# An attention and Fourier block: the Fourier stage's sums taken once for both halves of the frequencies, and one set of weight sums handed from VectorE to accumulating transfers

## The chip, the cores and the metric

The kernel runs on one core of a Trainium2 chip. A core has engines that run side by side, each with its own queue of instructions: TensorE (PE in the profile) multiplies matrices and writes to PSUM, which has eight banks of 128 partitions by 512 words; VectorE (DVE) and ScalarE (ACT) work element by element; GpSimd (POOL) and SyncE (SP) here mostly issue transfers (DMAs) between the chip's memory and the core's SBUF. The metric is the time of one execution on the device in microseconds (us): the median of several runs.

## The reference

One layer over 512 latent tokens of width 2048, with 256 context tokens:

```python
h = modulate(rmsnorm(x), shift, scale)          # shift, scale, gate from c @ w_ada
p = h @ w_in                                    # 2048 -> 9216
attn = attention(rope(q), [rope(k), kc], [v, vc])
u = u_b.reshape(b, n, 4, 128)                   # 4 groups of 128 channels
y = jnp.fft.fftn(u, axes=(1, 3), norm="ortho").real
y_a = (attn * silu(z_a)) @ w_pa
y_b = (y * silu(z_b)) @ w_pb
out = rmsnorm(x + gate * ((sigmoid(g_a) * y_a + sigmoid(g_b) * y_b) @ w_out)) * final_g
```

The edit is in the Fourier part (`u_b`, `z_b`) and at the start of the large product `h @ w_in`. Of the transform over 512 tokens and 128 channels only the real part is wanted. For a real input, the transforms at frequency f and at 512 − f of the tokens share their sums: with C the sum with cosines and S the sum with sines over the channels, one is C − S and the other C + S.

## The kernel before, in words

**Products in three.** All matmuls are done in single precision as three products of rounded parts. A weight tile of 128x1024 words is split by `split_from` (L181, L182): ScalarE copies it, rounded, into the high half (`hi`), and VectorE subtracts that from it for the low half (`lo`). `mm3` (L339 to L341) then issues high by high, high by low and low by high. The split of a tile must be done before its matmuls start; TensorE's order is fixed by the code in the stages spoken of here, and the order on the other engines is set by the scheduler of the framework, except where `issue_after` or `behind` names an instruction that must stand ahead. `look` says how many tiles are split ahead of their use.

**The stages.** A start stage, to about 144.5 us, makes the modulated rows of `h` and the columns of `u_b` and `z_b`. Then comes the channel stage (the Fourier part). Then the rest of `w_in` goes in eight groups, 0 to 7, each as seven products in the manner of Strassen, in the order P1, Q5, P2, Q6, P7, Q3, Q4. Each product has four pieces of 12 matmuls, 128x512 each: 48 in all.

**Sums of weights.** P1 needs the block A11 of the weights, Q5 the sum Z5, Q6 the sum S2: each one more addend on the one before. They are kept in four tiles, R0 to R3 (`chain`), one for each piece. A load on SP's queue fills R (L220) for P1. In `split_piece` (L263 and on) the next addend is put in one of two ways. Either the raw addend has been loaded into a buffer `wr`, and VectorE adds it (L269), when the piece is split; or a transfer on POOL's queue adds the addend from memory into R (L292, `accum_op=ALU.add`), as soon as the split before has read R. `BY_DVE_GATES = (1,)` says that step 1, Q5's sums, goes by VectorE; step 2, Q6's, by transfers. The loop over groups that fills the list of pieces hands it on at L429.

**The channel stage.** For each channel group g of four, `tokens(g)` multiplies the half-sums of `u` (`uh`, `ul`) with tables of cosines and sines over the tokens (`fsq`), once for even and once for odd frequencies, and splits the result into `ah`, `al`. `positions(g)` multiplies these with the channels' table `fch` (cos, −sin, sin): one PSUM bank gets 256 columns for the frequencies upward and 256, read backwards, for those downward, by 8 matmuls with `ah` (L940) and 4 with `al` (L943). VectorE multiplies the bank with the gate (L945). `gate_b(g)` makes the gate: ScalarE's Sigmoid of `z` (L950), and VectorE's product of the two (L951). While this goes on, pieces of P1 are split, held by `behind` after `low[g]`, the split of a channel group. The four results go to memory (`b_d`, L967) on POOL's queue. Behind these there, `turning <- rot_d` (L1394) loads the tables of rotations that the first group's queries need.

Of the kernel before, what the change touches and what calls it, by code (L numbers as in the profile page):

```python
# [18 lines left out]
P = 128  # L19
D = 2048  # L20
T = 512
# [25 lines left out]
HL, MORE_HL = 3, 2  # L47
EVEN = 258

# [74 lines left out]
def block_kernel(ctx, tc, xT, ctx_rows, ctx_toks, x, c_row, w_ss, w_gate, vecs, qkg, rope, dft_c, dft_s,  # L124
# [74 lines left out]
    def stream(key, src, *a, **k):  # L199
        todo.append(Piece(key, src if isinstance(src, list) else [src], *a, **k))  # L200
# [57 lines left out]

    last_split, split_of, in_line, context_sub = [], [], [], []

    look = [1]

    def split_piece(e):  # L263
# [27 lines left out]
        if e.nxt is not None:  # L291
            nc.gpsimd.dma_start(chain[e.pc], e.nxt, accum_op=ALU.add)  # L292
        if e.stage == 3:
# [74 lines left out]
    for p in start_pieces():  # L368
        if p[2:5:2] == (KK - 4, 0):
            stream(("dfts", 0), dft_s[:, : 2 * EVEN], 2 * EVEN, 2, "raw")  # L370
            stream(("dftc", 0), dft_c, 3 * P, 1, "raw")
        elif p[2:5:2] == (KK - 4, 4):
            stream(("dfts", 1), dft_s[:, 2 * EVEN :], T, 2, "raw")
        stream(("start", p), w_start[p[0] : p[0] + P * p[1]].rearrange("(p c) -> p c", p=P), p[1], p[2 + 1])
# [139 lines left out]
    with tc.issue_after(nc.scalar.activation(ce, cvt, ACT.Exp, scale=-1.0).ins):  # L514
# [381 lines left out]
    ul = fnp.tile([P, 2, 2, T], F32R, name="ul")  # L896
    fsq.append(fnp.tile([P, 2, 2, 256], F32R, name="fsq1"))
    split_table(1)
# [17 lines left out]

    AH, low = {}, {}

    def tokens(g):

        ah, al = (fnp.tile([P, 2, 257], F32R, tag=n, bufs=2, name=uid(n)) for n in ("ah", "al"))
        c = slice(P * g, P * g + P)
        for e in range(2):
            n = fsq[e].shape[-1]
            acc = bank()
            for a in range(2):
                mm3(acc[:, :n], uh[:, a, e, c], ul[:, a, e, c], fsq[e][:, 0, a, :], fsq[e][:, 1, a, :], a == 0, a == 1)
            k = slice(e, 257 - e, 2)
            low[g] = split_from(acc[:, :n].rearrange("p (r f) -> p r f", r=2), ah[:, :, k], al[:, :, k])[1]
        AH[g] = ah, al  # L930

    def positions(g):

        ah, al = AH.pop(g)
        acc = bank2()
        steps = [(256 * q, P * (r and 1 + q), (slice(0, 256) if q == 0 else slice(256, 0, -1)), r)
                 for q in range(2) for r in range(2)]
        for n, (o, t, k, r) in enumerate(steps):
            for m, i in enumerate((0, 1)):
                nc.tensor.matmul(acc[:, o : o + 256], fch[:, i, t : t + P], ah[:, r, k], start=n == m == 0, stop=False,  # L940
                                 skip_group_check=True)
        for n, (o, t, k, r) in enumerate(steps):
            nc.tensor.matmul(acc[:, o : o + 256], fch[:, 0, t : t + P], al[:, r, k], start=False, stop=n == 3,  # L943
                             skip_group_check=True)
        nc.vector.scalar_tensor_tensor(part[:, 4 + g, :], acc, 1.0 / 256.0, part[:, 4 + g, :], op0=ALU.mult, op1=ALU.mult)  # L945

    def gate_b(g):
        z = part[:, 4 + g, :]
        e = fnp.tile([P, T], F32, tag="sil", bufs=1, name=uid("e"))
        nc.scalar.activation(e, z, ACT.Sigmoid)  # L950
# [12 lines left out]
    ordered.close()  # L963
    look[0] = 2
# [428 lines left out]

    nc.gpsimd.dma_start(turning, rot_d)  # L1394
    for g, kind in enumerate(KINDS):
# [586 lines left out]
def _constants():  # L1982
# [9 lines left out]
    a = 2 * np.pi * (np.outer(np.arange(P), np.arange(P)) % P) / P  # L1992
    dft_c = np.concatenate([np.cos(a), -np.sin(a), np.sin(a)], axis=1).astype(np.float32)

# [4 lines left out]

    dft_s = np.concatenate([table(np.arange(0, T // 2 + 1, 2)), table(np.arange(1, T // 2, 2))], axis=1)  # L2000
    return np.ascontiguousarray(rope), np.ascontiguousarray(dft_c), np.ascontiguousarray(dft_s)
# [60 lines left out]
```

## Time and profile before

| | |
|---|---|
| median of 3 runs | 1290.95 us (1290.47 to 1291.25) |
| profiled execution | 1290.1 us, span 1288.3 us |
| granted TensorE clock, mean | 0.997 |
| TensorE busy | 1271.5 us (99%), 6586 matmuls |
| VectorE busy | 994.8 us (77%) |
| ScalarE busy | 681.1 us (53%) |
| POOL busy | 168.8 us (13%) |
| memory traffic | mean 248 GB/s |
| channel stage | 144.55 to 156.08 us |
| group 0 up to its last product | 156.08 to 223.31 us |

The span is the time from the first to the last record of the profiled execution; its own time includes what lies around that. A busy share of 99% means that nearly every microsecond has a matmul in flight; matmuls overlap, so the pace is read from the distance between starts. The rows give start, busy time, engine, line, operation and the tiles; in brackets stands the time that the engine idled before, and what ended the wait. Tile numbers are left out in the profile.

### The profile page before, as it was taken

The page shows a single profiled execution, that of the slowest core. Times are in us where ns is not written, and L with a number is a line of the kernel's source. Part 1 is how long each engine was busy: PE and PEld are TensorE (multiplying, and loading weights), DVE is VectorE, ACT ScalarE, POOL GpSimd, SP SyncE. Part 2 cuts the span into 40 slices and gives each one's busy share as a digit, 9 for nine tenths or more (in the row PEclk, how much of TensorE's full clock was granted, in tenths as well). Part 3 has the DMA queues.
Part 4 walks back from the last instruction along what each step waited for, and adds up shares of the span by engine and source line. Part 5 has one row for each costly group of instructions (what it writes and reads, how often), then busy time and mean ns, then how long its engine had stood idle before and what let it go on. Part 6 is the DMA issues. An engine that isn't in the chain of part 4 may idle for free.

```text
span 1288.3 us, 17679 instructions
## 1 busy us (share of the span) xinstructions
PE 1271.5 (99%) x6586; PEld 1047.1 (81%) x6586; DVE 994.8 (77%) x1305; ACT 681.1 (53%) x1072; POOL 168.8 (13%) x222
## 2 busy tenths in 40 slices
PE   8999999999999999999999999999999999999997
PEld 5677887888888888888888888888888888888886
DVE  5767899889779787758587666788898767887677
ACT  5322655645456455444354544666667646465544
POOL 0000011111102011012021010012100212211210
PEclk9999999999999999999999999999999999999999
DMA  9999588888899998977879897578852989898986
GB/s 377 411 367 345 207 216 251 246 212 250 210 310 253 297 269 262 294 191 189 271 212 265 284 229 258 182 245 241 267 179 77 248 244 259 243 213 229 225 201 180
DMA packets 104342, 319.14 MB, mean 248 GB/s; under 512 B 9888, under 2 KB 32800, under 8 KB 100288
## 3 DMA queue, kind: packets, MB, share of 16 engines
q1 hardware_dynamic: 54912, 197.40, 42.1%
q0 software_dynamic: 27024, 98.19, 35.6%
q10 hardware_dynamic: 22320, 22.42, 5.1%
q8 instruction: 51, 0.84, 0.2%
q14 instruction: 35, 0.29, 0.1%
HBM read 283.36 MB, written 34.61 MB: 247 GB/s over the span
## 4 chain that ended last, share of the span: by engine, by line
PE 90%; DVE 4%; DMA 3%; ACT 2%; issue 1%; SPq 0%; ACTq 0%; DVEq 0%
PE banks L339 10%; PE banks L340 10%; PE banks L341 10%; PE x L341 8%; PE x L339 8%; PE x L340 8%; PE y L341 7%; PE y L340 7%; PE y L339 7%; PE banks L1543 2%; PE pd L567 2%; PE pb L339 1%; PE pb L341 1%; PE pb L340 1%; PE pc L339 1%; DMA wa<-in_w_ss 1%
## 5 line engine op out<-in xcount | busy, mean ns | idle before, releaser
L181 ACT ACTIVATE whi<-R 128x1024 fp32r<-128x1024 f32 x138 | 145.1, 1058 | 138.7 <-PE banks L341 55.5
L182 DVE TENSOR_TENSOR wlo<-R,whi 128x1024 fp32r<-128x1024 f32 x138 | 167.2, 1220 | 54.4 <-ACT whi L181 54.0
L182 DVE TENSOR_TENSOR wlo<-wr,whi 128x1024 fp32r<-128x1024 f32 (+1 forms) x122 | 147.0, 1211 | 62.3 <-ACT whi L181 62.3
L181 ACT ACTIVATE whi<-wr 128x1024 fp32r<-128x1024 f32 (+1 forms) x122 | 127.4, 1051 | 127.8 <-PE y L341 39.2
L339 PE MATMUL banks<-whi,s 128*128 128x512 f32 (+1 forms) x400 | 157.8, 395 | 0.8 <-ACT ev L1154 0.7
L341 PE MATMUL banks<-whi,s 128*128 128x512 f32 (+1 forms) x400 | 155.9, 390 | 0.0
L340 PE MATMUL banks<-wlo,s 128*128 128x512 f32 (+1 forms) x400 | 155.8, 389 | 0.0
L339 PE MATMUL x<-whi,s 128*128 128x512 f32 x352 | 137.1, 390 | 0.0
L341 PE MATMUL x<-whi,s 128*128 128x512 f32 x352 | 137.0, 389 | 0.0
L340 PE MATMUL x<-wlo,s 128*128 128x512 f32 x352 | 136.9, 389 | 0.0
L339 PE MATMUL y<-whi,s 128*128 128x512 f32 x316 | 123.1, 389 | 0.2 <-DVE cxe L1266 0.2
L340 PE MATMUL y<-wlo,s 128*128 128x512 f32 x316 | 123.1, 389 | 0.1
L341 PE MATMUL y<-whi,s 128*128 128x512 f32 x316 | 122.8, 389 | 0.0
L292 POOL DMA_DIRECT2D R<-in_w_g x64 | 55.9, 873 | 418.8 <-DVE wlo L182 212.8
L181 ACT ACTIVATE s<-wr 128x512 fp32r<-128x512 f32 (+2 forms) x93 | 60.4, 676 | 74.1 <-DMA wr<-cf_d 24.9
L182 DVE TENSOR_TENSOR s<-wr,s 128x512 fp32r<-128x512 f32 (+2 forms) x93 | 66.8, 748 | 35.6 <-ACT s L181 34.7
L339 PEld LDWEIGHTS banks<-whi,s 128*128 128x128 f32 x400 | 75.2, 188 | 16.5 <-ACT ev L1154 1.1
L341 PEld LDWEIGHTS banks<-whi,s 128*128 128x128 f32 x400 | 75.1, 188 | 15.3
L340 PEld LDWEIGHTS banks<-wlo,s 128*128 128x128 f32 x400 | 75.2, 188 | 13.8 <-DVE wlo L182 0.2
L340 PEld LDWEIGHTS x<-wlo,s 128*128 128x128 f32 x352 | 66.1, 188 | 13.7
L341 PEld LDWEIGHTS x<-whi,s 128*128 128x128 f32 x352 | 66.1, 188 | 13.7
L339 PEld LDWEIGHTS x<-whi,s 128*128 128x128 f32 x352 | 66.1, 188 | 13.5
(322 smaller groups left out, 2796.6 us busy)
## 6 DMA issues: line engine op xcount, KB each, us to landing
wr<-in_w_g SPq DMA_DIRECT2D x128, 512.0 KB, 6.0
R<-in_w_g POOLq DMA_DIRECT2D x64, 512.0 KB, 7.7
wa<-in_w_ss SPq DMA_DIRECT2D x31, 1024.0 KB, 9.7
R<-in_w_g SPq DMA_DIRECT2D x32, 512.0 KB, 5.4
wr<-in_w_gate SPq DMA_DIRECT2D x32, 512.0 KB, 5.0
wr<-in_w_o SPq DMA_DIRECT2D x24, 512.0 KB, 7.2
R<-in_w_o POOLq DMA_DIRECT2D x24, 512.0 KB, 9.0
wr<-in_w_pab SPq DMA_DIRECT2D x20, 512.0 KB, 5.8
```

Source lines behind the costliest of these rows:

```text
L181: first = nc.scalar.activation(hi, src, ACT.Copy)
L182: return first, nc.vector.tensor_tensor(lo, src, hi.bitcast(F32), op=ALU.subtract)
L292: nc.gpsimd.dma_start(chain[e.pc], e.nxt, accum_op=ALU.add)
L339: nc.tensor.matmul(o, ah, bh, start=start, stop=False, skip_group_check=cont)
L340: nc.tensor.matmul(o, ah, bl, start=False, stop=False, skip_group_check=cont)
L341: nc.tensor.matmul(o, al, bh, start=False, stop=stop, skip_group_check=cont)
L567: nc.tensor.matmul(acc[32 * j : 32 * j + 32], c2[:, n, :], w[:, k, :], start=n < 4, stop=n >= KK - 4)
L1543: nc.tensor.transpose(tp[:, k * P : (k + 1) * P], p[:, k * P : (k + 1) * P], ident)
```

## The change

- Both token tables have 258 columns (`FREQ`); the odd one had 256.
- `positions` reads all 258 columns once: 3 matmuls into a bank for the sum with cosines, 3 into a second one for the sum with sines (6 in place of 12, each of 258 columns). ScalarE copies the second bank to `odd` (L941). VectorE forms the upward half as a difference (L942, 257 words), and the downward half as a sum of both read backwards (L943, 255 words, written from word 257 on) into `y`. The product with the gate follows later (L961), for two channel groups at a time. The factor 1/256 is in `fch`, which now holds cos and sin.
- The banks are exchanged: `tokens` writes to the tags `b2` and `b3` (two banks each, named `pd` and `pc`), `positions` to `b1` (four banks, `pb`).
- `gate_b` is one Silu on ScalarE (L948); the product of VectorE is gone.
- In group 0, Q5's sums go by accumulating transfers on POOL's queue (L292); their raw loads and VectorE's sums (L269) go there.
- The rotations' load (L1415) is issued in group 0's P2, after the last accumulating transfer issued until then (`chained`).
- For the last two channel groups, pieces are held behind `low[3]`.

```diff
-EVEN = 258
+FREQ = 258
...
         if e.nxt is not None:
-            nc.gpsimd.dma_start(chain[e.pc], e.nxt, accum_op=ALU.add)
+            chained[:] = [nc.gpsimd.dma_start(chain[e.pc], e.nxt, accum_op=ALU.add)]
...
-            stream_product(name, g, w_g[g], BY_DVE_GATES)
+            stream_product(name, g, w_g[g], BY_DVE_GATES if g else ())
...
-    fch = ppool.tile([P, 2, 3 * P], F32R, name="fch")
-    fsq = [ppool.tile([P, 2, 2, EVEN], F32R, name="fsq0")]
+    fch = ppool.tile([P, 2, 2 * P], F32R, name="fch")
+    fsq = [ppool.tile([P, 2, 2, FREQ], F32R, name="fsq0")]
...
-        ah, al = (fnp.tile([P, 2, 257], F32R, tag=n, bufs=2, name=uid(n)) for n in ("ah", "al"))
+        ah, al = (fnp.tile([P, 2, FREQ], F32R, tag=n, bufs=2, name=uid(n)) for n in ("ah", "al"))
...
-            acc = bank()
+            acc = (bank3 if e else bank2)()[:, :FREQ]
...
-        acc = bank2()
-        steps = [(256 * q, P * (r and 1 + q), (slice(0, 256) if q == 0 else slice(256, 0, -1)), r)
-                 for q in range(2) for r in range(2)]
-        for n, (o, t, k, r) in enumerate(steps):
-            for m, i in enumerate((0, 1)):
-                nc.tensor.matmul(acc[:, o : o + 256], fch[:, i, t : t + P], ah[:, r, k], start=n == m == 0, stop=False,
+        acc = [bank()[:, :FREQ] for _ in range(2)]
+        for i, v in ((0, ah), (1, ah), (0, al)):
+            for r, o in enumerate(acc):
+                nc.tensor.matmul(o, fch[:, i, P * r : P * r + P], v[:, r, :], start=i == 0 and v is ah, stop=v is al,
                                  skip_group_check=True)
-        for n, (o, t, k, r) in enumerate(steps):
-            nc.tensor.matmul(acc[:, o : o + 256], fch[:, 0, t : t + P], al[:, r, k], start=False, stop=n == 3,
-                             skip_group_check=True)
-        nc.vector.scalar_tensor_tensor(part[:, 4 + g, :], acc, 1.0 / 256.0, part[:, 4 + g, :], op0=ALU.mult, op1=ALU.mult)
+        z = part[:, 4 + g, :]
+        y, odd = (fnp.tile([P, n], F32, tag=t, bufs=4, name=uid(t)) for t, n in (("y", T), ("odd", FREQ)))
+        nc.scalar.copy(odd, acc[1])
+        nc.vector.tensor_tensor(y[:, :257], acc[0][:, :257], odd[:, :257], op=ALU.subtract)
+        nc.vector.tensor_tensor(y[:, 257:], acc[0][:, 255:0:-1], odd[:, 255:0:-1], op=ALU.add)
+        products.append((z, y))
 
     def gate_b(g):
         z = part[:, 4 + g, :]
-        e = fnp.tile([P, T], F32, tag="sil", bufs=1, name=uid("e"))
-        nc.scalar.activation(e, z, ACT.Sigmoid)
-        nc.vector.tensor_tensor(z, z, e, op=ALU.mult)
+        nc.scalar.activation(z, z, ACT.Silu)
...
-        with behind((finals[-1], low[g])):
+        with behind((finals[-1], low[g if g < 2 else 3])):
             for e in ahead[:g]:
                 split_piece(e)
+            for z, y in products[2 * g - 4 : 2 * g - 2] if g > 1 else ():
+                nc.vector.tensor_tensor(z, y, z, op=ALU.mult)
...
-    nc.gpsimd.dma_start(turning, rot_d)
...
+            if (g, name) == (0, "P2"):
+                with behind(chained):
+                    nc.gpsimd.dma_start(turning, rot_d)
```

Three places in the order of the instructions, of the kernel before and of the changed one. The first is VectorE's, at the end of the channel stage, up to the low half of R3 (`wlo` from R3, P1's fourth piece). `wlo` and `s` are low halves, `Z50`, `Z51` and `S30` are forms of the tokens' rows, `pd` and `pb` PSUM banks. Before:

```order
L182 TENSOR_TENSOR wlo272_1596<-R2_1341,whi271_1595 128x1024
L945 SCALAR_TENSOR_TENSOR part_108<-pd266_1560,part_108 128x512
L269 TENSOR_TENSOR R0_1339<-R0_1339,wr230_1353 128x1024
L945 SCALAR_TENSOR_TENSOR part_108<-pd270_1581,part_108 128x512
L182 TENSOR_TENSOR s280_1667<-Z50_69,s279_1666 128x1024
L182 TENSOR_TENSOR s284_1689<-Z51_70,s283_1688 128x1024
L269 TENSOR_TENSOR R1_1340<-R1_1340,wr231_1359 128x1024
L269 TENSOR_TENSOR R2_1341<-R2_1341,wr238_1405 128x1024
L182 TENSOR_TENSOR wlo278_1651<-R3_1342,whi277_1650 128x1024
```

and with the change:

```order
L961 TENSOR_TENSOR part_108<-y250_1482,part_108 128x512
L961 TENSOR_TENSOR part_108<-y258_1516,part_108 128x512
L942 TENSOR_TENSOR y274_1576<-pb272_1568,odd275_1577 128x257
L943 TENSOR_TENSOR y274_1576<-pb272_1568,odd275_1577 128x255
L182 TENSOR_TENSOR wlo277_1582<-R2_1341,whi276_1581 128x1024
L961 TENSOR_TENSOR part_108<-y268_1555,part_108 128x512
L961 TENSOR_TENSOR part_108<-y274_1576,part_108 128x512
L182 TENSOR_TENSOR s284_1654<-Z50_69,s283_1653 128x1024
L182 TENSOR_TENSOR s289_1677<-Z51_70,s288_1676 128x1024
L182 TENSOR_TENSOR s302_1745<-S30_67,s301_1744 128x1024
L182 TENSOR_TENSOR wlo282_1637<-R3_1342,whi281_1636 128x1024
```

The three sums at L269 are gone from this stretch, the low half of `S30`, which stood five rows behind R3's, now stands ahead of it, and the products at L961 stand among the low halves.

The second place is POOL's queue of transfers, from the store of the rotations' tables on. Before:

```order
L767 DMA rot_d_77<-S30_67 128x1024
L967 DMA b_d_80<-part_108 128x1024 x2
L1394 DMA qr_1617<-rot_d_77 128x1024
L292 DMA R0_1339<-in_w_g 128x1024
L292 DMA R1_1340<-in_w_g 128x1024
L292 DMA R2_1341<-in_w_g 128x1024
L292 DMA R3_1342<-in_w_g 128x1024
```

and with the change:

```order
L767 DMA rot_d_77<-S30_67 128x1024
L292 DMA R0_1339<-in_w_g 128x1024
L292 DMA R1_1340<-in_w_g 128x1024
L966 DMA b_d_80<-part_108 128x1024
L292 DMA R2_1341<-in_w_g 128x1024
L966 DMA b_d_80<-part_108 128x1024
L292 DMA R3_1342<-in_w_g 128x1024
L292 DMA R0_1339<-in_w_g 128x1024
L292 DMA R1_1340<-in_w_g 128x1024
L292 DMA R2_1341<-in_w_g 128x1024
L292 DMA R3_1342<-in_w_g 128x1024
L1415 DMA qr_1606<-rot_d_77 128x1024
```

The rotations' load (into `qr`) stood ahead of the first accumulating transfer, and stands behind the eighth; four accumulating transfers are new, and stand between the stores of the channel stage.

The third is VectorE's again, at the end of the start stage (`fsq1` is the odd table, `wr280` a raw weight of P2). Before:

```order
L182 TENSOR_TENSOR fsq1_1348<-wr199_1139,fsq1_1348 128x512
L660 TENSOR_TENSOR part_108<-pc232_1361,part_108 128x512
L904 TENSOR_TENSOR u2233_1375<-pb43_296,part_108 128x512
L904 TENSOR_TENSOR u2234_1379<-pb43_296,part_108 128x512
L660 TENSOR_TENSOR part_108<-pc235_1383,part_108 128x512
```

and with the change:

```order
L182 TENSOR_TENSOR fsq1_1348<-wr199_1139,fsq1_1348 128x516
L182 TENSOR_TENSOR s40_287<-wr280_1634,s38_286 128x2x256
L182 TENSOR_TENSOR s72_434<-wr280_1634,s70_433 128x2x256
L660 TENSOR_TENSOR part_108<-pc230_1357,part_108 128x512
L904 TENSOR_TENSOR u2231_1371<-pb43_296,part_108 128x512
L904 TENSOR_TENSOR u2232_1375<-pb43_296,part_108 128x512
```

The two low halves of a P2 piece, which stood behind P1's last low half before, come ahead of the channel stage; those of a second one (`s97`, `s128`) come among the first splits of `al` in the same way.

More of the change, by code (lines that the diff above doesn't have):

```diff
@@ L369, in block_kernel @@
         if p[2:5:2] == (KK - 4, 0):
-            stream(("dfts", 0), dft_s[:, : 2 * EVEN], 2 * EVEN, 2, "raw")
-            stream(("dftc", 0), dft_c, 3 * P, 1, "raw")
+            stream(("dfts", 0), dft_s[:, : 2 * FREQ], 2 * FREQ, 2, "raw")
+            stream(("dftc", 0), dft_c, 2 * P, 1, "raw")
         elif p[2:5:2] == (KK - 4, 4):
-            stream(("dfts", 1), dft_s[:, 2 * EVEN :], T, 2, "raw")
+            stream(("dfts", 1), dft_s[:, 2 * FREQ :], 2 * FREQ, 2, "raw")
         stream(("start", p), w_start[p[0] : p[0] + P * p[1]].rearrange("(p c) -> p c", p=P), p[1], p[2 + 1])
@@ L896, in block_kernel @@
     ul = fnp.tile([P, 2, 2, T], F32R, name="ul")
-    fsq.append(fnp.tile([P, 2, 2, 256], F32R, name="fsq1"))
+    fsq.append(fnp.tile([P, 2, 2, FREQ], F32R, name="fsq1"))
     split_table(1)
@@ L915, in block_kernel @@
         pass
-    AH, low = {}, {}
+    AH, low, products = {}, {}, []
     def tokens(g):
-        ah, al = (fnp.tile([P, 2, 257], F32R, tag=n, bufs=2, name=uid(n)) for n in ("ah", "al"))
+        ah, al = (fnp.tile([P, 2, FREQ], F32R, tag=n, bufs=2, name=uid(n)) for n in ("ah", "al"))
         c = slice(P * g, P * g + P)
         for e in range(2):
-            n = fsq[e].shape[-1]
-            acc = bank()
+            acc = (bank3 if e else bank2)()[:, :FREQ]
             for a in range(2):
-                mm3(acc[:, :n], uh[:, a, e, c], ul[:, a, e, c], fsq[e][:, 0, a, :], fsq[e][:, 1, a, :], a == 0, a == 1)
-            k = slice(e, 257 - e, 2)
-            low[g] = split_from(acc[:, :n].rearrange("p (r f) -> p r f", r=2), ah[:, :, k], al[:, :, k])[1]
+                mm3(acc, uh[:, a, e, c], ul[:, a, e, c], fsq[e][:, 0, a, :], fsq[e][:, 1, a, :], a == 0, a == 1)
+            k = slice(e, FREQ, 2)
+            low[g] = split_from(acc.rearrange("p (r f) -> p r f", r=2), ah[:, :, k], al[:, :, k])[1]
         AH[g] = ah, al
@@ L1998, in table @@
         return v.reshape(2, P, -1).transpose(1, 0, 2).reshape(P, -1)
-    dft_s = np.concatenate([table(np.arange(0, T // 2 + 1, 2)), table(np.arange(1, T // 2, 2))], axis=1)
+    dft_s = np.concatenate([table(np.arange(e, FREQ, 2)) for e in range(2)], axis=1)
     return np.ascontiguousarray(rope), np.ascontiguousarray(dft_c), np.ascontiguousarray(dft_s)
```

4 lines of the change are left out of this document (2 added, 2 removed).

## The prediction, made before the run

> **What bounds the kernel now.** I read the page first, then TensorE's waits between 140 and 230 us, then a table of busy time by stage, then the timelines of the engines around the edit. The page says what sets the end:
>
> ```profile
> span 1288.3 us, 17679 instructions
> PE 1271.5 (99%) x6586; PEld 1047.1 (81%) x6586; DVE 994.8 (77%) x1305; ACT 681.1 (53%) x1072; POOL 168.8 (13%) x222
> PE x L340 <- DVE s L182: 0.7, 1, 0.7
> PE y L341 <- DVE s L182: 0.2, 1, 0.2
> ```
>
> TensorE is busy for 99%, so a change is worth the matmul time that it takes out, plus waits of TensorE that go, less waits that come. The last two lines are the only named waits from 140 to 230 us: both end when VectorE (DVE) has written the low half of a weight (L182). The stages from the channel stage to the end of the first group's sixth product (columns: window, its length, PE, PEld, DVE, ACT, POOL busy, clock, DMA share, GB/s):
>
> ```profile
> 144.50:156.10 11.60, 11.60 (x98) 11.56 (x98) 11.41 (x21) 8.71 (x16) 0.53 (x1) 1.00 0.20 80
> 156.10:167.00 10.90, 10.90 (x51) 9.02 (x50) 10.77 (x11) 5.60 (x7) 1.27 (x3) 1.00 0.68 218
> 200.00:212.00 12.00, 11.31 (x50) 9.05 (x49) 12.00 (x16) 5.38 (x7) 2.15 (x3) 1.00 0.75 199
> 212.00:223.30 11.30, 11.06 (x49) 8.81 (x48) 11.10 (x12) 6.03 (x7) 0.00 (x0) 1.00 0.93 318
> ```
>
> The reader is to see two full columns: TensorE and VectorE are both without slack here. Matmuls taken from the first row are a gain only as far as VectorE keeps up.
>
> **TensorE's part of the change.** Rows of its timeline (start, busy, name, count):
>
> ```profile
> 144.55 0.28 PE L339 MATMUL pb<-fsq,uh 128*128 128x258 f32 x1
> 147.42 1.12 PE L940 MATMUL pd<-ah,fch 128*128 128x256 f32 x8
> 148.38 0.64 PE L943 MATMUL pd<-al,fch 128*128 128x256 f32 x4
> 156.08 0.40 PE L339 MATMUL x<-whi,s 128*128 128x512 f32 x1
> 164.48 0.39 PE L340 MATMUL x<-wlo,s 128*128 128x512 f32 x1
> 166.97 0.39 PE L339 MATMUL y<-whi,s 128*128 128x512 f32 x1
> 172.41 0.39 PE L339 MATMUL y<-whi,s 128*128 128x512 f32 x1
> 172.91 0.50 PE L340 MATMUL y<-wlo,s 128*128 128x512 f32 x1
> 208.18 0.39 PE L339 MATMUL x<-s,s 128*128 128x512 f32 x1
> 209.25 0.50 PE L340 MATMUL x<-s,s 128*128 128x512 f32 x1 [0.69 <-DVE s L182]
> 209.59 0.40 PE L341 MATMUL x<-s,s 128*128 128x512 f32 x1
> 212.10 0.39 PE L340 MATMUL y<-s,s 128*128 128x512 f32 x1
> 212.73 0.50 PE L341 MATMUL y<-s,s 128*128 128x512 f32 x1 [0.24 <-DVE s L182]
> 223.31 0.39 PE L339 MATMUL x<-s,s 128*128 128x512 f32 x1
> ```
>
> Eight 256-column matmuls start over 147.42 to 148.38, so one costs 0.120 us. `positions` falls from 12 to 6 of them in four channel groups: 24 × 0.12 = 2.88 us out; the 258-column forms cost two columns more in 24 left and 24 of `tokens`, under 0.1. The stage takes 156.08 − 144.55 = 11.53 now and 8.75 then, so the first product, P1, starts at about 153.3.
>
> A 512-column matmul costs (166.97 − 156.08)/48 = 0.227 us; after a wait the next one starts 0.34 later (209.25 to 209.59). Before loses time three times to low halves: at 172.41 (0.50 + 0.34 instead of 2 × 0.227: 0.39), at 208.18 (1.07 + 0.34: 0.96) and at 212.10 (0.63 + 0.34: 0.51), 1.86 in all. From P1's start to 223.31 six products take 67.23 where 6 × 10.886 = 65.32 would do, which confirms it (1.91).
>
> **VectorE's part.** Its rows, and two of ScalarE's:
>
> ```profile
> 144.08 1.28 DVE L182 TENSOR_TENSOR ul<-u,uh 128x512 fp32r<-128x512 f32 x2
> 145.28 0.68 DVE L660 TENSOR_TENSOR part<-pc,part 128x512 f32<-128x512 f32 x1
> 146.48 0.75 DVE L182 TENSOR_TENSOR al<-pb,ah 128x258 fp32r<-128x258 f32 x2
> 147.93 0.75 DVE L182 TENSOR_TENSOR al<-pb,ah 128x258 fp32r<-128x258 f32 x2
> 148.60 1.21 DVE L182 TENSOR_TENSOR wlo<-R,whi 128x1024 fp32r<-128x1024 f32 x1
> 149.73 0.68 DVE L945 SCALAR_TENSOR_TENSOR part<-pd,part 128x512 f32<-128x512 f32 x1
> 155.93 1.22 DVE L269 TENSOR_TENSOR R<-R,wr 128x1024 f32<-128x1024 f32 x1
> 157.06 0.68 DVE L945 SCALAR_TENSOR_TENSOR part<-pd,part 128x512 f32<-128x512 f32 x1
> 157.66 2.35 DVE L182 TENSOR_TENSOR s<-Z,s 128x1024 fp32r<-128x1024 f32 x2
> 162.41 1.23 DVE L182 TENSOR_TENSOR wlo<-R,whi 128x1024 fp32r<-128x1024 f32 x1
> 146.65 0.63 ACT L950 ACTIVATE e<-part 128x512 f32<-128x512 f32 x1
> 147.19 0.84 ACT L181 ACTIVATE ah<-pb 128x258 fp32r<-128x258 f32 x2
> ```
>
> By distance from start to start, one of 1024 words takes 1.13 us (155.93 to 157.06), of 512 words 0.60 (157.06 to 157.66), of 258 words 0.335 (two from 147.93 to 148.60). Removed: four sums at L269 (4.52), four products at L951 and four at L945 (4.80). Added: eight halves of `y` at 0.335 (2.68) and four products at L961 (2.40). That is 4.2 us less. But the order of the changed kernel puts four early low halves (`s40`, `s72`, `s97`, `s128`, 0.60 each, 2.40) ahead of the first group, and the low half of `S30` (1.13) ahead of that of R3, P1's fourth piece. So up to R3 VectorE has only 4.24 − 3.53 = 0.7 less to do, while TensorE comes 2.8 earlier.
>
> Stepped through: up to 145.28 I keep the rows of before (ScalarE's `uh` sets them). `s97` and `s128` stand where products at L951 stood, at the same 0.60. The second `al` can wait 0.5 for ScalarE, since its `ah` now stands behind a 512-word Silu (146.65 to 147.19 in before). So R0's low half starts at 148.6 to 149.1; I take 149.1. From there without a gap: R0 1.13, eight halves of 258 words (two `y` pairs, two `al` pairs) 2.68, R1 1.13, a `y` pair 0.67, two products 1.20, a `y` pair 0.67, R2 1.13, two products 1.20, three of 1024 words 3.39, together 13.2. R3's low half starts at 162.3 and ends at 163.5, as good as before (162.41).
>
> TensorE wants it at 153.3 + 36 × 0.227 + 0.227 = 161.7. **So 1.9 us of the 2.8 turn into a wait at P1's fourth piece**, and the second product, Q5, starts at 163.6 + 0.34 + 10 × 0.227 = 166.2, against 166.97: 0.76 gained. Bounds: no wait at all (gain 2.8 there), or, with `y` at the price of a 512-word row, 8 × 0.265 = 2.1 more of wait.
>
> Behind R3 VectorE is ahead: four halves of 512 words and two operations of 1024 (the fourth sum, `S30`), 2.40 + 2.26 = 4.66 us, are gone from what followed. Q5 begins only 0.76 earlier, so every later low half has some 3.9 us more than before, and the three stalls (at most 0.96 long) go. With five gapless products Q4 starts at 166.2 + 54.4 = 220.6 against 223.31: **2.7 us gained**. Behind that the order of all engines is the same but for group 3.
>
> **The transfers.** The first group's Q5 sums leave VectorE for four accumulating transfers (L292) on POOL's queue; each waits for the low half of its R, and the rotations' load goes behind eight of them.
>
> ```profile
> 166.81 0.90 POOL L292 DMA_DIRECT2D R<-in_w_g  x1 [3.65 <-DVE wlo L182]
> R<-in_w_g POOLq DMA_DIRECT2D x1, 512.0 KB, 5.5
> DMA to landing us min/median/max: 9.2/9.9/12.4
> 162.62 0.55 POOL L1394 DMA_DIRECT2D qr<-rot_d  x1 [4.04 <-ACT whi L181]
> qr<-rot_d POOLq DMA_DIRECT2D x1, 512.0 KB, 6.6
> 193.76 0.68 DVE L1210 TENSOR_TENSOR qr<-x,qr 128x512 f32<-128x512 f32 x1
> ```
>
> The second line is one transfer with little beside it (issued at 188.5), the third the four issued from 166.8 to 174.3 with loads running beside them. R3's is issued at 163.6; Q5's fourth piece starts at 166.2 + 36 × 0.227 = 174.4, less 0.95 for ScalarE's copy and 1.2 for the low half: it must land by 172.2, that is within 8.6 us. Q5 needs no weight loads any more, and P2's are asked for earlier, so I expect little beside it and take a value nearer 5.5 than 9.9: hidden. If that cover is gone, it costs 1.3 (9.9) to 3.8 (12.4). The rotations' load would be issued at about 175 and land 6.6 later, at 182; its first reader is at 193.76: nothing. The banks exchanged, the product later and the smaller tables cost nothing by themselves.
>
> **Silu for Sigmoid.** It saves VectorE's product (counted) and costs one more table load in group 3, ahead of the first Sigmoid there. ScalarE's rows:
>
> ```profile
> 138.51 1.28 ACT L950 ACT_TABLE_LOAD   x1
> 422.06 1.07 ACT L181 ACTIVATE whi<-wr 128x1024 fp32r<-128x1024 f32 x1 [1.18 <-PE y L341]
> 424.78 1.06 ACT L181 ACTIVATE whi<-wr 128x1024 fp32r<-128x1024 f32 x1 [1.65 <-PE y L341]
> ```
>
> 1.28 us, where ScalarE idles 1.18 and 1.65 waiting for TensorE: hidden, at most 0.2 without that.
>
> The sum: 2.8 less matmul time − 1.9 new wait − 0.1 rounding + 1.9 old stalls = 2.7. The profiled execution took 1290.1 (span 1288.3 and 1.8 around it): 1287.4. The median of the runs is 0.85 above it, so I predict 1290.95 − 2.7 = **1288.3 us**.
>
> **A rule that speaks against it.** Writing the second half of `y` reads both sources backwards and starts at an odd word (257). The Trainium skill, page "Vector Engine (DVE) Microarchitecture Reference", section "Measured stream behaviour on trn2", says that a port streams at full rate only in runs of two or more adjacent words that begin on an 8-byte boundary; it measured 1.30 ns a column for pairs at odd words and 1.75 for small steps, against 1.05, and no step of −1. By that, as an estimate, four times 255 columns would cost 0.25 to 0.7 ns more each, 0.3 to 0.7 us of wait at R3. The row of `al` disagrees in part: ScalarE's `ah` and `al` are read and written at every second word there, and 258 of them still take 0.335, just the line through 512 (0.60) and 1024 (1.13).
>
> **The rivals.**
> 1. *VectorE keeps up at P1's fourth piece.* For it: some of its rows may start earlier when eight operations leave it. Against it: the 13.2 us above have no gap to close. Gain 2.8 + 1.9 = 4.6: 1286.3. Chance 0.08.
> 2. *The backward halves are slow.* For it: no row reads backwards. Against it: the `al` row. At the 512-word price R3 comes 2.1 later: gain 0.6, 1290.4; at half of that 1289.4. Chance 0.10. In a small form the four backward halves cost a quarter to a half more than 0.335, together 0.3 to 0.7 of wait at R3: gain 2.0 to 2.4, 1288.6 to 1289.0, chance 0.08. This is what the skill's rule on adjacent pairs would do here.
> 3. *R3's transfer is late*, on the other side. For it: the four rows of 9.2 to 12.4, and three more transfers now follow on the same queue within 8 us. Against it: 5.5 alone. At 9.9 a stall of 1.3 at Q5's fourth piece: 1289.6, chance 0.10. From 8.6 + 2.7 = 11.3 us to landing the kernel is slower than before; at 12.4 the stall of 3.8 eats all: 1292.1. Chance 0.06.
>
> **The numbers.** The forecast has 0.58, with its own range 1287.4 to 1289.2 (R0 from 148.6 on, a stall of before left, a slip of 0.5 in Q5). The range 1286.3 to 1290.6 takes in all but late transfers and the tails. 0.2%, 2.6 us, is about what a measurement of this kernel can tell from no change, and the forecast lies on that line: 0.34 of its 0.58 count as faster, with rival 1 this makes 0.42. Slower by over 2.6 us needs rival 3 beyond its longest row, or a mishap of another kind: 0.06. The rest, 0.52, is no difference.
>
> **What would show it.** In the trace after: 72 matmuls in the channel stage and P1's start near 153.3; one wait of 1.5 to 2 us of TensorE at P1's fourth piece, ended by R3's low half near 163.5; Q5 near 166.2; no stalls near 172, 208 and 212 (or 2.7 earlier); Q4 near 220.6, and a constant offset behind it. `y`'s two rows should show 0.335 from start to start. The prediction is wrong if the wait at R3 is missing or above 3, if a wait of TensorE ends with a transfer into R in Q5, or if the offset changes between group 1 and the end.

## The result: 2.2 us faster, and where the trace put it

| | before | after |
|---|---|---|
| median | 1290.47 us (1289.56 to 1291.25, 22 runs) | 1288.24 us (1287.27 to 1290.01, 22 runs) |
| profiled execution's span | 1288.3 us | 1286.6 us |
| mean granted clock | 0.997 | 0.998 |

The ratio is 0.9985, with a 95% interval of 0.9979 to 0.9991: 1.2 to 2.7 us faster. The forecast, 1288.3 us and 2.7 us less than before, has its time right; its gain lies at the upper end of the interval. That the time agrees to 0.1 us is partly luck: the gain was 0.4 us smaller than forecast, and the kernel before came out 0.48 us lower here than the 1290.95 us the forecast started from.

The profile after, first TensorE's timeline (start, busy, engine, line, operation, tiles; in brackets the wait ahead and what ended it): the channel stage's first matmul, `positions` of the first channel group in two rows, P1's first matmul, the two around its wait, Q5's and Q4's first ones.

```profile
144.44 0.28 PE L339 MATMUL pd<-fsq,uh 128*128 128x258 f32 x1
147.34 0.65 PE L937 MATMUL pb<-ah,fch 128*128 128x258 f32 x4
147.83 0.40 PE L937 MATMUL pb<-al,fch 128*128 128x258 f32 x2
153.18 0.39 PE L339 MATMUL x<-whi,s 128*128 128x512 f32 x1
161.38 0.39 PE L339 MATMUL x<-whi,s 128*128 128x512 f32 x1
163.36 0.50 PE L340 MATMUL x<-wlo,s 128*128 128x512 f32 x1 [1.58 <-DVE wlo L182]
166.00 0.39 PE L339 MATMUL y<-whi,s 128*128 128x512 f32 x1
220.43 0.39 PE L339 MATMUL x<-s,s 128*128 128x512 f32 x1
```

The channel stage takes 153.18 − 144.44 = 8.74 us, against 11.53. At P1's fourth piece the distance from one start to the next is 1.98 instead of 0.227. Behind that the products run without a gap: from Q5 to Q4 54.43 us for five of 10.886. Q4 starts 2.88 us before its place in the kernel before (223.31).

VectorE's timeline up to that wait:

```profile
148.75 1.22 DVE L182 TENSOR_TENSOR wlo<-R,whi 128x1024 fp32r<-128x1024 f32 x1
149.89 0.42 DVE L942 TENSOR_TENSOR y<-pb,odd 128x257 f32<-128x257 f32 x1
150.22 0.42 DVE L943 TENSOR_TENSOR y<-pb,odd 128x255 f32<-128x255 f32 x1
150.55 0.42 DVE L182 TENSOR_TENSOR al<-pd,ah 128x258 fp32r<-128x258 f32 x1
...
158.68 2.35 DVE L182 TENSOR_TENSOR s<-Z,s 128x1024 fp32r<-128x1024 f32 x2
160.95 1.22 DVE L182 TENSOR_TENSOR s<-S,s 128x1024 fp32r<-128x1024 f32 x1
162.09 1.22 DVE L182 TENSOR_TENSOR wlo<-R,whi 128x1024 fp32r<-128x1024 f32 x1
```

The first row is R0's low half, the last R3's. Between them VectorE has no gap worth naming: 13.3 us. The backward half of `y` (L943) starts at 150.22 and its successor at 150.55: 0.33 us for 255 words, as for the forward half.

POOL's and ScalarE's timeline, and the answer on the eight accumulating transfers issued from 150 to 176 us (from issue to landing):

```profile
163.60 0.86 POOL L292 DMA_DIRECT2D R<-in_w_g  x1 [3.97 <-DVE wlo L182]
174.64 0.87 POOL L1415 DMA_DIRECT2D qr<-rot_d  x1
171.22 1.06 ACT L181 ACTIVATE whi<-R 128x1024 fp32r<-128x1024 f32 x1 [1.01 <-DMA R<-in_w_g]
415.85 1.28 ACT L1181 ACT_TABLE_LOAD   x1
```

```profile
DMA to landing us min/median/max: 5.7/7.4/7.9
```

R3's transfer, issued at 163.60, landed at about 171.2, when ScalarE's copy could start. The table load in group 3 takes 1.28 us, and TensorE shows no wait near it.

The lead of 2.88 us at Q4 is 1.7 us at the end of the span. So some 1.2 us are lost behind group 0, where the prediction expected none to be.

### The profile page after: what moved, and what is told of

Same layout as the page of the kernel before. It is cut to its first block, busy times and chain, and to the rows that moved or that the text cites. A ratio compares the mean times of both kernels' runs of the same rounds, so it can differ in the third digit from the quotient of the medians.

```text
span 1286.6 us, 17643 instructions
## 1 busy us (share of the span) xinstructions
PE 1269.8 (99%) x6562; PEld 1045.1 (81%) x6562; DVE 991.0 (77%) x1305; ACT 683.3 (53%) x1077; POOL 173.0 (13%) x226
## 4 chain that ended last, share of the span: by engine, by line
PE 90%; DMA 4%; DVE 3%; ACT 2%; issue 1%; SPq 0%; ACTq 0%; DVEq 0%
PE banks L339 10%; PE banks L340 10%; PE banks L341 10%; PE x L340 9%; PE x L341 9%; PE x L339 9%; PE y L339 7%; PE y L340 7%; PE y L341 7%; PE banks L1544 2%; PE pd L567 2%; PE pc L339 1%; PE pc L341 1%; PE pc L340 1%; PE pb L339 1%
## 5 line engine op out<-in xcount | busy, mean ns | idle before, releaser
L292 POOL DMA_DIRECT2D R<-in_w_g x68 | 59.4, 873 | 488.7 <-DVE wlo L182 222.3
```

The lines of the kernel that those rows point to most:

```text
L292: chained[:] = [nc.gpsimd.dma_start(chain[e.pc], e.nxt, accum_op=ALU.add)]
```

## The experiments

The theory going in: VectorE's queue, not TensorE's own work, sets the first group's time; the matmuls saved are worth only as much as low halves come earlier. Its rivals: the parts add up by TensorE's work; the transfers set the time; the order on POOL's and ScalarE's queues is of no account. "Q4's lead" below is how much earlier than 223.31, the kernel before, that run's profile has the first matmul of Q4 in group 0. It is read from one execution, the profiled one. A median is set beside the median of the kernel before, run on the same chip at the same time; it is of 10 to 12 executions, of 22 in the first row and of only 5 in the row "the same, copy later".

| kernel | Q4's lead, us | median, us | before, us | ratio (95%) |
|---|---|---|---|---|
| the change | 2.88 | 1288.24 | 1290.47 | 0.9985 (0.9979 to 0.9991) |
| the change, again | 2.73 | 1288.83 | 1290.24 | 0.9989 (0.9981 to 0.9998) |
| sums once alone | −1.78 | 1292.02 | 1290.46 | 1.0011 (1.0002 to 1.0020) |
| transfers alone | −2.78 | 1291.09 | 1290.46 | 1.0008 (0.9999 to 1.0017) |
| transfers alone, one order mended | 2.00 | 1287.94 | 1290.61 | 0.9979 (0.9970 to 0.9987) |
| banks not exchanged | 1.36 | 1290.11 | 1290.61 | 0.9994 (0.9985 to 1.0002) |
| rotations' load early | −3.02 | 1293.76 | 1290.61 | 1.0024 (1.0015 to 1.0033) |
| S30 behind R3 | 3.13 | 1288.03 | 1290.46 | 0.9979 (0.9970 to 0.9988) |
| three forms behind R3 | 3.63 | 1287.49 | 1290.46 | 0.9977 (0.9968 to 0.9986) |
| the same, copy later | 4.28 | 1286.16 | 1290.61 | 0.9963 (0.9951 to 0.9975) |
| copy later alone | 2.90 | 1288.99 | 1290.24 | 0.9989 (0.9980 to 0.9997) |
| a longer wait at R3 | 1.76 | 1290.26 | 1290.24 | 0.9998 (0.9989 to 1.0007) |

### One part at a time: the sums alone

```diff
-            stream_product(name, g, w_g[g], BY_DVE_GATES if g else ())
+            stream_product(name, g, w_g[g], BY_DVE_GATES)
...
+    nc.gpsimd.dma_start(turning, rot_d)
     for g, kind in enumerate(KINDS):
...
-            if (g, name) == (0, "P2"):
-                with behind(chained):
-                    nc.gpsimd.dma_start(turning, rot_d)
```

> The changed kernel with Q5's sums back on VectorE and the rotations' load early; the Fourier stage's sums once. Theory (VectorE's queue sets the first group): P1 starts near 153.3, 2.8 earlier, but R3's low half ends only at 164.1 to 165.2, so TensorE waits 2.5 to 3.6 us at P1's fourth piece, Q5 starts at 166.8 to 167.9 against 166.97 in the kernel before, and the later stalls stay. Gain between -0.9 and 0.3 us: the 24 matmuls saved are worth nothing. Rival (the parts add up): gain 2.0 to 2.8 us.

Its timeline at P1's fourth piece, and its busy times by stretch (window, length, then PE, PEld, DVE, ACT, POOL busy, granted clock, DMA share, GB/s):

```profile
162.48 0.45 PE L339 MATMUL x<-whi,s 128*128 128x512 f32 x1
165.63 0.57 PE L340 MATMUL x<-wlo,s 128*128 128x512 f32 x1 [2.71 <-DVE wlo L182]
166.00 0.63 PE L341 MATMUL x<-whi,s 128*128 128x512 f32 x1
166.43 0.63 PE L339 MATMUL x<-whi,s 128*128 128x512 f32 x1
```

```profile
156.00:162.00 6.00, 6.00 (x28) 4.98 (x27) 6.00 (x9) 4.57 (x6) 1.06 (x2) 1.00 0.43 171
166.00:168.00 2.00, 2.00 (x6) 1.61 (x5) 2.00 (x3) 0.00 (x0) 0.38 (x1) 0.50 0.54 213
```

P1 began at 154.30, 1.8 us before its place in the kernel before but 1.0 later than expected, and Q5 at 169.85, 2.9 us behind its place there. R3's low half ended at 165.6, a little behind the 164.1 to 165.2 expected, and the wait was 2.7 us. What was not expected came behind the wait: the next matmuls are 0.43 us apart, at a granted clock of 0.50, for some 3.4 us, which costs 1.6 us more. Q4 starts 1.8 us late, and the kernel is slower than before (its interval reaches from 0.02% to 0.20%). Without the fall of the clock Q4 would stand 0.2 us late. The rival, that the 24 matmuls count by themselves, is out: their 2.8 us do not show.

### One part at a time: the transfers alone

```diff
-            nc.gpsimd.dma_start(chain[e.pc], e.nxt, accum_op=ALU.add)
+            chained[:] = [nc.gpsimd.dma_start(chain[e.pc], e.nxt, accum_op=ALU.add)]
...
-            stream_product(name, g, w_g[g], BY_DVE_GATES)
+            stream_product(name, g, w_g[g], BY_DVE_GATES if g else ())
...
-    nc.gpsimd.dma_start(turning, rot_d)
...
+            if (g, name) == (0, "P2"):
+                with behind(chained):
+                    nc.gpsimd.dma_start(turning, rot_d)
```

> The kernel before with only the transfers edited: Q5's sums of the first group by accumulating transfers, the rotations' load behind them; the Fourier stage as before. Theory (VectorE's queue sets the first group): the channel stage stays 11.5 us and P1 starts near 156; 3.4 us of sums leave VectorE ahead of R3's low half, 1.7 us of other low halves come in, so that half ends near 161.9, 2.6 before TensorE wants it; the three later stalls (1.9 us) go. Gain 1.9 us. Rival (the parts add up by TensorE's own work): no matmul is taken out, so no more than 0.3 us.

A miss: 1291.09 us, no faster than before. R3's low half ended at 162.75 and P1 ran through, but Q5 stopped at its third piece (timeline, TensorE and VectorE):

```profile
172.83 0.39 PE L339 MATMUL y<-whi,s 128*128 128x512 f32 x1
175.85 0.79 PE L340 MATMUL y<-wlo,s 128*128 128x512 f32 x1 [2.63 <-DVE wlo L182]
176.44 0.63 PE L341 MATMUL y<-whi,s 128*128 128x512 f32 x1
173.43 1.23 DVE L277 TENSOR_TENSOR wr<-R,wr 128x1024 f32<-128x1024 f32 x1 [3.06 <-DMA R<-in_w_g]
174.58 2.35 DVE L182 TENSOR_TENSOR wlo<-R,whi 128x1024 fp32r<-128x1024 f32 x2
```

With VectorE freer, the scheduler had put the first difference of P7's weights (L277) ahead of R2's low half. It needs R0 after its second accumulating transfer, issued only at 165.92; VectorE waits 3.06 us for it, with two low halves behind, whose high halves were ready. And again the clock falls behind the wait: the matmuls after 176.44 come 0.43 apart. This fall was seen in the profiled execution, of 1291.79 us; the median is 1291.09, so it need not be in every one.

### The transfers alone, that order mended

```diff
+                if e.key[1] == 0:
+                    line.enter_context(tc.issue_after(fourth[0].ins))
                 nc.vector.tensor_tensor(src, chain[e.pc], src, op=ALU.subtract)
```

(`fourth` holds the low half of Q5's fourth piece.)

> The kernel with only the transfers edited, and one wait more: VectorE's differences of P7's weights in group 0 stand behind the low half of Q5's fourth piece. Theory: what made that kernel slower was the first of these differences, which stood ahead of R2's low half and waited for R0's second accumulating transfer; without it no wait is left at Q5's third piece, the clock does not fall, the three stalls of the kernel before are gone, and the gain over the kernel before is 1.5 to 1.9 us (over its first form 4 us in the trace). Rival: the transfers themselves are late (one of 9 us among them), the wait stays at Q5's third or fourth piece, and it is no faster than the kernel before.

1287.94 us, ratio 0.9979. No wait of TensorE is left between 140 and 225 us, P1 starts at 156.02 and Q4 at 221.31, 2.00 ahead (TensorE's timeline, the lines shifted by four):

```profile
156.02 0.40 PE L343 MATMUL x<-whi,s 128*128 128x512 f32 x1
221.31 0.39 PE L343 MATMUL x<-s,s 128*128 128x512 f32 x1
```

So the transfers were not late, the order was. And this half of the change, with one wait moved, is worth as much as the whole: the three stalls of the kernel before (1.9 us) are what it takes away. The sums taken once add 0.9 us to Q4's lead, from 2.00 to 2.88. In the medians they add nothing that can be seen: 2.7 us less than before here, 2.2 and 1.4 with the whole change.

### The banks not exchanged

```diff
-            acc = (bank3 if e else bank2)()[:, :FREQ]
+            acc = bank()[:, :FREQ]
...
-        acc = [bank()[:, :FREQ] for _ in range(2)]
+        acc = [bank2()[:, :FREQ] for _ in range(2)]
```

> The changed kernel with the banks as before: the tokens' products in the four banks, the positions' pairs in the two. Theory: each pair of banks must be read by VectorE before the next positions start, TensorE waits about 1.2 us ahead of the second and 2.2 ahead of the fourth, P1 starts at 156.3 to 156.6, R3's low half comes in time, Q5 starts at 167.2 to 167.5 and Q4 at 221.7: the gain over the kernel before is 1.4 us, half of the changed kernel's. Rival (the exchange costs nothing, as the prediction had it, since VectorE sets the time at R3): Q5 starts at 166.0 all the same.

TensorE's timeline:

```profile
150.87 0.60 PE L937 MATMUL pd<-ah,fch 128*128 128x258 f32 x3 [1.01 <-DVE y L943]
155.99 0.60 PE L937 MATMUL pd<-ah,fch 128*128 128x258 f32 x3 [1.24 <-DVE y L943]
156.66 0.40 PE L339 MATMUL x<-whi,s 128*128 128x512 f32 x1
```

P1 starts at 156.66, no wait is left at R3, and Q4's lead is 1.36, close to what the theory had. Its waits were sized less well: 1.01 and 1.24 us instead of 1.2 and 2.2, and one of 0.46 at 154.36 for ScalarE's copy into `odd` (L941) that it did not have. The exchange is worth 1.5 us at Q4.

### The rotations' load early

```diff
+    nc.gpsimd.dma_start(turning, rot_d)
     for g, kind in enumerate(KINDS):
...
-            if (g, name) == (0, "P2"):
-                with behind(chained):
-                    nc.gpsimd.dma_start(turning, rot_d)
```

> The changed kernel with the rotations' load issued early, where it stands ahead of R3's first accumulating transfer on POOL's queue and waits for its buffer until 162.6 or later. Theory: R3's transfer is issued at 164 to 165 instead of 163.6, shares the engines with 512 KB more, and lands 1 to 2.5 us later than 171.2; 0.6 us of slack are there, so TensorE waits 0.5 to 2 us at Q5's fourth piece and the gain over the kernel before falls to between 1 and 2.4 us. Rival (the place of this load is of no account): no wait in Q5.

The timelines of POOL, ScalarE and TensorE in this run:

```profile
168.01 0.55 POOL L1393 DMA_DIRECT2D qr<-rot_d  x1 [8.14 <-DMA b_d<-part]
168.55 2.71 POOL L292 DMA_DIRECT2D R<-in_w_g  x3
176.24 1.06 ACT L181 ACTIVATE whi<-R 128x1024 fp32r<-128x1024 f32 x1 [5.78 <-DMA R<-in_w_g]
177.35 0.50 PE L339 MATMUL y<-whi,s 128*128 128x512 f32 x1 [2.75 <-ACT whi L181]
```

The direction was right, the size was not: a median of 1293.76, 3.2 above the kernel before. The load waits for a store of the channel stage to land (8.14 us on POOL, to 168.0, not to 162.6), three accumulating transfers stand behind it, R3's lands 5 us later, TensorE waits 2.75 and then 0.76 us at Q5's fourth piece, and the clock falls once more (next matmuls 0.43 apart). Q4 is 3.0 us later than before the change, 5.9 later than with the load in its place.

### VectorE's order at R3

One wait more, on VectorE: the low half of the form behind that of R3.

```diff
-        split_from(src, hi, lo)
+        first = nc.scalar.activation(hi, src, ACT.Copy)
+        with tc.issue_after(fourth[0].ins) if turn_fm[0] in (10, 12) else nullcontext():
+            nc.vector.tensor_tensor(lo, src, hi.bitcast(F32), op=ALU.subtract)
```

(Here `fourth` is the low half of P1's fourth piece; 10 and 12 mean the two halves of S3. The second kernel has 6 and 8 too, the two halves of Z5.)

> The changed kernel with one wait more on VectorE: the low half of the form S30 stands behind the low half of R3. Theory: R3's low half starts 1.13 us earlier, at 160.95, the wait of 1.75 us at P1's fourth piece falls to 0.6, Q5 starts at 164.9, and the gain over the changed kernel is 1.1 us. Rival (another thing holds Q5, a transfer into R or the copies on ScalarE): the wait moves into Q5 and the gain is under 0.3 us.

> The changed kernel with the low halves of Z50, Z51 and S30 all behind R3's low half. Theory: R3's low half starts at 158.7, nothing waits at P1's fourth piece, Q5 starts at 164.1, R0's low half for Q5 ends at 162.1 in time; gain over the changed kernel 1.7 to 1.9 us, over the kernel before 3.7 to 4.5. Rival: Q5's R2 or R3, still in flight or waiting for a buffer of halves, takes the time back: gain over the changed kernel under 0.5 us with a wait of TensorE at Q5's third or fourth piece.

With S30 behind, R3's low half starts at 161.36 and TensorE's wait falls from 1.58 to 0.49 (VectorE's and TensorE's timeline):

```profile
161.36 1.22 DVE L182 TENSOR_TENSOR wlo<-R,whi 128x1024 fp32r<-128x1024 f32 x1
153.58 0.40 PE L341 MATMUL x<-whi,s 128*128 128x512 f32 x1
162.62 0.50 PE L342 MATMUL x<-wlo,s 128*128 128x512 f32 x1 [0.49 <-DVE wlo L182]
```

Q4's lead grows by 0.25 only, since 0.5 us are lost at Q5's third piece. With all three behind, nothing waits in P1 and Q5 starts at 164.24, but the third piece loses 0.84. The timelines of ScalarE, VectorE and TensorE in that second run:

```profile
167.35 1.02 ACT L1117 COPY ev<-x 128x1024 f32<-128x1024 f32 x1 [4.58 <-DMA b_d<-part]
169.36 1.23 DVE L182 TENSOR_TENSOR wlo<-R,whi 128x1024 fp32r<-128x1024 f32 x1 [1.31 <-ACT whi L181]
170.63 0.50 PE L342 MATMUL y<-wlo,s 128*128 128x512 f32 x1 [0.57 <-DVE wlo L182]
```

So both theory and rival were right in part: the wait at R3 is VectorE's order, and a second wait stands close behind it. The medians of both runs have intervals that overlap the change's, so it is the traces that tell them apart. ScalarE's copy of P1's result waits 4.58 us for a buffer that a store of the channel stage is still reading; R2's copy stands behind it.

### That copy later

```diff
+                elif self.g == 0:
+                    after(3, lambda: nc.scalar.copy(self.X, a))
                 else:
                     nc.scalar.copy(self.X, a)
```

> The changed kernel with the forms' low halves behind R3's, and ScalarE's copy of P1's result in group 0 three pieces later, behind the copy of R2 for Q5. Theory: the 0.84 us lost at Q5's third piece in the run with the forms behind came from that copy, which waits on ScalarE's queue for a store of the channel stage to land, with R2's copy behind it; without it nothing waits from P1 to Q4, Q4 starts at 218.8 to 219.0, and the gain over the kernel before is 4.4 to 4.6 us at Q4. Rival: R2's accumulating transfer lands too late by itself and the wait stays within 0.3 us of what it was.

> The changed kernel with only ScalarE's copy of P1's result moved behind the copy of R2 for Q5; the forms' low halves stay where they are. Theory: as long as VectorE holds TensorE 1.6 us at P1's fourth piece, the copy is covered and moving it is worth nothing: the same Q5 start (166.0) and Q4 (220.4), within 0.2. Rival: it is worth its 0.6 us alone too.

The timelines of ScalarE and TensorE in the run with the forms behind R3 as well:

```profile
165.61 1.06 ACT L181 ACTIVATE whi<-R 128x1024 fp32r<-128x1024 f32 x1 [3.06 <-DVE wlo L182]
166.84 1.02 ACT L1117 COPY ev<-x 128x1024 f32<-128x1024 f32 x1 [0.17 <-DMA b_d<-part]
164.01 0.39 PE L341 MATMUL y<-whi,s 128*128 128x512 f32 x1
219.03 0.39 PE L341 MATMUL x<-s,s 128*128 128x512 f32 x1
```

R2's copy is now ahead, Q5 runs through, Q4's lead is 4.28; one wait of 0.31 in Q3 keeps it below 4.4. The median is 1286.16, ratio 0.9963 (0.9951 to 0.9975): faster than both kernels, its interval clear of the change's (0.9979 to 0.9991), though from five executions only. By itself the same copy is worth nothing (lead 2.90, ratio 0.9989), as long as R3 holds TensorE anyway.

### How long a wait the clock bears

R3's low half late by one short row and one sum of 512 words:

```diff
+                    nc.vector.tensor_tensor(lo[:, :64], src[:, :64], hi[:, :64].bitcast(F32), op=ALU.subtract)
                     last_split.append((f, nc.vector.tensor_tensor(lo, src, hi.bitcast(F32), op=ALU.subtract)))
```

> The changed kernel with R3's low half later on VectorE: 64 of its words are written twice and a sum of 512 words comes between, 0.14 + 0.60 us, so the wait at P1's fourth piece is 2.3 us instead of 1.6. Theory (the clock of TensorE falls once a wait is long enough, as behind 2.6, 2.7 and 2.8 us, not behind 1.6): if the limit lies below 2.3, the next 7 or so matmuls come 0.43 apart and Q5 starts 0.7 + 1.2 to 1.7 us later than 166.0; if above, at 166.7 with the clock at 1.00. Rival (the fall has another cause than the length of the wait): no fall at 2.3 and no order with the length.

TensorE's timeline around the wait (the lines are shifted by six):

```profile
161.78 0.39 PE L345 MATMUL x<-whi,s 128*128 128x512 f32 x1
164.53 0.50 PE L346 MATMUL x<-wlo,s 128*128 128x512 f32 x1 [2.36 <-DVE wlo L292]
164.87 0.40 PE L347 MATMUL x<-whi,s 128*128 128x512 f32 x1
```

After 2.36 us of waiting the pace is 0.23 at once and the clock 1.00. With the falls behind 2.63, 2.71 and 2.75 the limit would lie between 2.4 and 2.6 us, if the length of the wait alone decides; each length was seen once. That it does isn't shown. The ten executions of this kernel lie in two groups of five, 1288.5 to 1290.0 us (mean granted clock 0.998) and 1290.6 to 1291.3 us (0.994 to 0.997), and the profiled one (1289.09) is in the first. A fall behind this wait in the second group would fit the 1.9 us between the groups' medians. But none of that group was profiled, and the mean clock doesn't settle it, as it also depends on the first 20 us: they are granted 1.00 in the change's profile and 0.83 in its second one. The median of all ten, 1290.26, lies between the groups and is no better than before, although Q4's lead in the profile is 1.76; the first group's median is 1.15 us below the kernel before.

### The change a second time, and where 1.2 us went behind group 0

> The changed kernel itself, a second execution under the profile. Theory: up to Q4 it repeats its first trace within 0.2 us (wait of 1.6 us at R3, Q4 2.7 to 2.9 ahead of the kernel before); of the 1.2 us that its first trace lost behind Q4, most is the lateness of single transfers, which differs from one execution to the next, so the lead at the end differs from 1.5 by 0.4 or more, either way. Rival: the same waits stand at the same places again, and the lead at the end is 1.5 within 0.2.

Up to Q4 it repeats itself: a wait of 1.6 us at R3, lead 2.73. Behind that it does not. This time 0.96 us are lost in Q3 of group 4, at 524 us, where the first execution lost nothing. On ScalarE a row that stands ahead of Q3's splits waits for a load of the context's forms (`cf_d`) on SP's queue. Its timeline in the first execution of the change:

```profile
518.33 1.15 ACT L181 ACTIVATE s<-wr 128x512 fp32r<-128x512 f32 x2 [6.37 <-DMA wr<-cf_d]
```

and in this one, with TensorE's row:

```profile
519.75 1.15 ACT L181 ACTIVATE s<-wr 128x512 fp32r<-128x512 f32 x2 [5.73 <-DMA wr<-cf_d]
524.03 0.50 PE L340 MATMUL y<-wlo,s 128*128 128x512 f32 x1 [0.67 <-DVE wlo L182]
```

The load lands 1.4 us later. At the end of the span 0.7 us are left of 2.73, against 1.7 of 2.88 in the first execution. So the losses behind group 0 differ by 0.8 us between two executions of one kernel, and what they end on at 524 us is a load. Another place is common to both, at 1122 us, where TensorE waits for a load of `yb_d` (line 1658); the kernel before has no such wait. The waits of the first and the second execution:

```profile
PE banks L1658 <- DMA s<-yb_d: 0.2, 1, 0.2
PE banks L1658 <- DMA s<-yb_d: 0.9, 1, 0.9
```

That single transfers' luck accounts for all of them isn't shown: over 33 runs of the change the median gain (2.2 and 1.4 us) stays below the lead at Q4, so some part is there each time.

## Why the prediction was right, and where it was not

- *TensorE's sum.* 8.75 us for the channel stage were forecast, 8.74 came; P1 at 153.3, and it was 153.18. The six products take 10.886 each when nothing waits.
- *VectorE's steps.* R0's low half at 149.1: 148.75. Then 13.2 us without a gap: 13.3. R3's at 162.3: 162.09. The new wait of 1.9: 1.98 − 0.227 + 0.1 (the 0.33 behind it) = 1.86. Q5 at 166.2: 166.00. Q4 at 220.6: 220.43. The three old stalls went. One sum beside these steps is wrong: "0.7 less to do" up to R3 takes off four sums of 1.13 us, but only three of them stood ahead of R3's low half (the fourth starts at 164.16, the low half at 162.41), and the prediction counts the fourth again behind R3. With three it is 0.4 us more to do. The forecast doesn't use this sum; it goes by the rows in their order. Apart from that sum this part of the prediction holds step by step, and the runs that reorder VectorE's queue show the cause: R3's low half 0.73 us earlier and P1 0.40 later took 1.09 off the wait, three forms behind it took all.
- *Which part pays.* The prediction set 2.8 us less matmul time against 1.9 of new wait, and called the 1.9 us of old stalls the rest. The runs with one part say the same from the other side: the sums alone slow the kernel, the transfers alone, with one order mended, give 2.0 us at Q4. A claim behind it failed: in the expectations the transfers alone were to give their gain as they stood, and an order of the scheduler's took it away.
- *The transfers.* "A value nearer 5.5 than 9.9: hidden": hidden it was, but R3's took 7.5, with others in flight beside it, and R3's copy waited 1.01 us for it. Of the 8.6 us allowed, 1.1 were left; by the trace the cover was thinner, since R3's low half for Q5 ended at 173.8, 0.6 us before its matmul (166.00 + 37 × 0.227 = 174.4).
- *What was costed at nothing.* The table load and the second half of `y` cost nothing, as said; rival 2 falls: 0.33 us for 255 words backwards from an odd word. The Trainium skill's page "Vector Engine (DVE) Microarchitecture Reference" (section "Measured stream behaviour on trn2") has no step of −1 among its rows; its price for pairs at odd words or small steps (1.75 ns a column for steps of 72 or 152 words, and 2.50 for 24, which the prediction left out) does not apply here. The exchange of banks and the late rotations' load cost nothing in the change, but each is a condition: 1.5 and 5.9 us without it.
- *A rival that was missing.* The wait made by the change is 1.58 us, and behind waits of 2.6 to 2.8 us the profiles show 1.3 to 1.6 us more, by the clock. The prediction priced longer waits at their length alone, so its rivals 2 and 3 were too cheap on the slow side. The Trainium skill, page "TensorE: Matmul & The Clock Gate", section "What's actually happening", says that the clock halves after an idle window of about 3.4 us, free-running; in the profiles here it halved behind 2.63 us and not behind 2.36, so the waits seen here were shorter than that rule's window.
- *"A constant offset behind it."* The step that failed in size: the lead of 2.88 at Q4 was to hold to the end and be the gain, and a changing offset was one of the prediction's own signs of being wrong. The spans keep 1.7 of it, the medians 2.2 and 1.4. The loss in the profile begins at 620 us (2.43 at 638), on a row of VectorE (`cxe`, L1265) whose queue had waited for ScalarE's split of a load of `cf_d`, and goes on in the last stages; the second execution lost at 524 us already. The term missing from the sum is a price for what is lost behind group 0, 0.6 to 1.3 us by the medians; the places looked at end on loads, but that loads are all of it isn't shown.

## What to carry to other kernels

Where two engines are full in a stage, matmuls taken from one are worth only as much as the other can follow; count the other's queue in order, row by row, up to the row that is waited for. Freeing an engine lets the scheduler reorder it: look for a row that waits on a transfer and now stands ahead of rows that are ready. The same holds for the queues of ScalarE (a copy waiting on a store) and POOL (a load waiting ahead of accumulating transfers): what stands behind the waiting row is the price, and it was 0.8 and 5.9 us here.

## What the runs showed of the hardware

In the profiles TensorE's clock falls to half (0.50 to 0.51 granted, 0.43 us from start to start instead of 0.227) behind waits of 2.63, 2.71 and 2.75 us, for 2.7 to 3.4 us, and not behind 1.58 or 2.36 us. Where it falls, 1.3 to 1.6 us come on top of the wait. Whether a given length always brings the fall isn't shown. VectorE reads 255 words backwards from two sources, one of them in PSUM, and writes them from an odd word on, in the same 0.33 us as 257 words forwards.
